# The FFN norms of a macaron transformer block: sums over features by products with ones, in place of transposes

## The chip, the cores and the metric

The kernel runs on one core of a Trainium2 chip. A time is the device time of one execution in microseconds (us). Three runs of the kernel before took 961.36, 961.11 and 961.50 us; their median is 961.36 us. One further execution was profiled, and all rows shown come from it.

In the rows, PE is TensorE's matrix products and PEld its weight loads, DVE is VectorE, ACT is ScalarE, POOL is GpSimd and SP is SyncE, which issues most transfers. L106 is line 106 of the kernel.

## The reference

The input is one sequence of 512 tokens with 1024 features in float32. The block is a "macaron": half an FFN, a mixer with two kinds of sparse attention, half an FFN, and a last norm.

```python
def rmsnorm(x, g):
    y = x * rsqrt(mean(x * x, axis=-1) + 1e-6)
    return y * g

def swiglu(h, w_gate, w_up, w_down):          # 1024 -> 2816 -> 1024
    return (silu(h @ w_gate) * (h @ w_up)) @ w_down

x = x + 0.5 * swiglu(rmsnorm(x, norm_ffn1), w_ffn1_gate, w_ffn1_up, w_ffn1_down)
x = x + hybrid_mixer(rmsnorm(x, norm_mix), ...)
x = x + 0.5 * swiglu(rmsnorm(x, norm_ffn2), w_ffn2_gate, w_ffn2_up, w_ffn2_down)
out = rmsnorm(x, norm_final)
```

The change concerns the first and the third `rmsnorm`, those ahead of the two FFNs.

## The kernel before

**Layout.** The activations stay on the chip as eight tiles `xs[k]` of 128 features x 512 tokens: features lie on the partitions, tokens along the free dimension. A sum over features, which a norm needs, is therefore a sum over eight tiles and then over 128 partitions.

**Precision.** Every matrix product is made from halves: a float32 operand is split into `hi`, the value rounded to the type float32r by ScalarE (a copy), and `lo`, the rest, by a subtraction on VectorE. `mm3` (lines 105 to 109) then makes three products, hi by hi (L106), hi by lo (L107) and lo by hi (L108); `mm2` makes two where one operand is exact. Weights are split in `halves` (hi at L95, lo at L99), the plain FFN blocks into `whi` and `wlo` with five buffers each.

**The norm.** The gain of the norm goes into the activations when they are split (`gained`, L162 and L163). The factor of each token, one over the root of the mean square, is applied behind the product, since it is the same for all features. `squares` (L175 to L179) squares each tile on ScalarE and adds the squares on VectorE into `acc`, 128 x 512, which still has to be summed over partitions. `rms` does that: four transposes of 128x128 on TensorE (L192) into the PSUM tile `pr`, so that tokens lie on partitions; a sum along the free dimension on VectorE (L193) into `rc`, 128x4; root on ScalarE (L194) and reciprocal on VectorE (L195) on these 128x4 values; four more transposes (L198), of `rc` spread over 128 columns, into the PSUM tile `pR`; and a copy by ScalarE (L200) into `R`, 128 x 512, where every partition holds the factors of all 512 tokens. `rms` is called three times: for both FFN norms and for the mixer's, which also uses `rc` itself.

**The FFN.** The 2816 hidden features are 22 blocks of 128. The first four (f = 0 to 3) are computed by `plain`: per block a product with the gate's weights (m = 0) and one with the up weights (m = 1), each of eight steps k of three products, 24 products of 128x512 into one PSUM tile `pgu`. `finish` multiplies both by R (L312), takes silu (L313), multiplies (L314) and splits the result into `h` (`kept`, L281 and L282). The 18 other blocks are computed in pairs by a Winograd scheme of seven half-width products (`pair`), whose right-hand operands are sums of blocks of the normed x; `sums_of_x` (L238 to L243) and `blocks_of_x` make them on VectorE and ScalarE from `xs` and R while TensorE works on the plain blocks. `down` makes the products back to 1024 features, group by group, between the others.

**What sets the order.** The kernel is written with a tile framework that plans the order of each engine's instructions at build time with a simulated timeline and priorities; the engines then run their own queues in that order and wait on semaphores. `tc.high_priority()` raises a block's priority in the planner. `tc.issue_after(ins)` makes what the block contains, on the engine of `ins`, stand behind `ins` in that engine's queue. `go` runs through the list of steps and calls a stage's parts with different leads. The norm's places are set by `rms_at`, which maps a step (f, m, k) to an instruction that it has to stand behind: the product of f = 1, m = 0, k = 4 stands behind the last transpose of `acc`, and the first product of m = 1 behind the last transpose of `rc`. In the first FFN `rms` is called in `after(0)`, behind the first product of the FFN and `squares`; in the second one also in `after(0)`, while the squares of x are made by the mixer's last job (`w_out`).

PSUM has eight banks, used as four tags (s, t, o, mm) of two buffers each; `pt(None, ...)` takes the four tags in turn. The SBUF tag `h` has 16 buffers. `wake` (L621 to L625) is a dozen products of a matrix of ones with itself at the very start, which keep TensorE at work until data arrive; the ones are set by VectorE in float32 and cast to float32r (L621).

Of the kernel before, what the change touches and what calls it, by code (L numbers as in the profile page):

```python
# [9 lines left out]
F32 = mybir.dt.float32  # L10
F32R = mybir.dt.float32r
AF = mybir.ActivationFunctionType
ALU = mybir.AluOpType
AX = mybir.AxisListType

S = 512
D = 1024
# [12 lines left out]
def block_kernel(ctx: ExitStack, tc: tile.TileContext, A: dict, out: bass.AP):  # L30
# [7 lines left out]
    nc = tc.nc  # L38

    cp = ctx.enter_context(tc.tile_pool(name="cp", bufs=1))  # L40
# [7 lines left out]
    def pt(tag, name):  # L48

        if tag is None:  # L50
            tag = ("s", "t", "o", "mm")[turns[0] % 4]
            turns[0] += 1
        return ps.tile([128, S], F32, name=name, tag=tag, bufs=2)

    def f32(ap):
        return ap.bitcast(F32)
# [62 lines left out]
    def mm2(p, w, v, first, last):  # L119

        nc.tensor.matmul(p, w, v[0], start=first, stop=False)
        return nc.tensor.matmul(p, w, v[1], start=False, stop=last)
# [17 lines left out]
    eps = cp.tile([128, 1], F32, name="eps")  # L140
# [6 lines left out]
    tabs = cp.tile([33, 16], F32, name="tabs")  # L147
    far = cp.tile([32, 16], F32, name="far")
    cp.tile([128, 48], F32, name="rest")
    ones_f = cp.tile([128, 128], F32, name="ones_f")  # L150
    nc.vector.memset(ones_f, 1.0)
    ident = cp.tile([128, 128], F32, name="ident")
    make_identity(nc, ident)

# [1 line left out]
    made = [None]  # L156
# [10 lines left out]
    R = cp.tile([128, S], F32, name="R")  # L167
    rc = cp.tile([128, NT], F32, name="rc")

    acc = cp.tile([128, S], F32, name="acc")  # L170
# [11 lines left out]
    summed = [None]  # L182
    turned_R, copied_R = [None], [None]

    def rms(ptag):


        with tc.high_priority():
            p = pt(ptag, "pr")
            for i in range(NT):  # L190
                b = slice(i * 128, (i + 1) * 128)
                summed[0] = nc.tensor.transpose(p[:, b], acc[:, b], ident)  # L192
            nc.vector.tensor_reduce(rc, p.rearrange("p (i n) -> p i n", i=NT), AX.X, ALU.add)  # L193
            nc.scalar.activation(rc, rc, AF.Sqrt, bias=eps, scale=1.0 / D)  # L194
            nc.vector.reciprocal(rc, rc)  # L195
            p = pt(ptag, "pR")
            for i in range(NT):
                turned_R[0] = nc.tensor.transpose(p[:, i * 128:(i + 1) * 128],  # L198
                                                  rc[:, i:i + 1].to_broadcast([128, 128]), ident)
            copied_R[0] = nc.scalar.activation(R, p, AF.Copy)  # L200


    HT = S // 2

    class Ffn:
# [14 lines left out]
        def __init__(self, wg, wu, which, tmp, hp, sp):  # L220
            self.w, self.which, self.tmp, self.hp, self.sp = (wg, wu), which, tmp, hp, sp
            self.xg, self.hs, self.steps = None, {}, []
            self.b, self.temps = {}, {}
            self.last_lo = None
            self.x_made = None
            self.waiting = []
            self.in_pair = None
            self.runs, self.left = 0, 0
            self.rms_at = {}
            self.th, self.tl = [sp.tile([128, 4, 3, HT], F32R, name=n, tag=n, bufs=1) for n in ("th3", "tl3")]  # L230
            sp.tile([128, 16], F32, name="gap", tag="gap", bufs=1)

# [52 lines left out]
        def plain(self, f):  # L285

            got = {}

            def loads(m):
                if first_w:  # L290
                    got[m] = first_w.pop(0)
                else:
                    got[m] = chunk((8, 128))
                    fetch(got[m], self.w[m][f])

            def halves_of(m):
                with tc.issue_after(self.x_made.ins) if self.x_made and m else nullcontext():
                    got[m] = halves(got[m])
                if self.x_made and m:
                    self.x_made, self.first_up = None, last_hi[0]  # L300

            def run(m):
                p = got["p", m] = pt(None, "pgu")
                for k in range(NK):
                    gate = self.rms_at.get((f, m, k))
                    with tc.issue_after(gate[0].ins) if gate else nullcontext():
                        mm3(p, got[m][k], self.xg[k], k == 0, k == NK - 1)

            def finish():
                t = [self.t("t") for _ in range(2)]  # L310
                for m in range(2):
                    nc.vector.tensor_tensor(t[m], got["p", m], R, ALU.mult)  # L312
                self.silu = nc.scalar.activation(t[0], t[0], AF.Silu)  # L313
                nc.vector.tensor_tensor(t[1], t[1], t[0], ALU.mult)  # L314
                self.kept(f, t[1])

            return [[lambda m=m: loads(m), None, lambda m=m: halves_of(m), lambda m=m: run(m), finish if m else None]
                    for m in range(2)]

# [294 lines left out]
    with ExitStack() as ph:  # L614
        tmp = ph.enter_context(tc.tile_pool(name="tmp1", bufs=5))
        hp = ph.enter_context(tc.tile_pool(name="hp1", bufs=2))
        sp = ph.enter_context(tc.tile_pool(name="sp1", bufs=2))


        ones = hp.tile([128, S], F32R, name="ones", tag="h", bufs=16)[:, :128]  # L620
        nc.vector.tensor_copy(ones, ones_f)  # L621
        wake = pt(None, "wake")
        for _ in range(12):
            nc.tensor.matmul(wake.rearrange("p (a b) -> p a b", a=4), ones,
                             ones.unsqueeze(1).to_broadcast([128, 4, 128]), start=True, stop=True)  # L625
        nc.scalar.activation(R[:, 0:1], eps, AF.Sqrt)
        ffn = Ffn(A["wg1"], A["wu1"], 0, tmp, hp, sp)
        ffn.xg = [gained(k, 0) for k in range(NK)]
        ffn.x_made = made[0]
        ffn.rms_at = {(1, 0, 4): summed, (1, 1, 0): turned_R}  # L630

        make_rows = bias_rows(hp)

        def after(i):
            if i == 0:
                with tc.issue_after(ffn.first_up.ins):
                    for k in range(NK):
                        squares(hp, k, "h", 16)
                rms(None)
            if i == 3:  # L640
                make_rows()
            if 3 <= i < 7:
                ffn.sums_of_x(i - 3)
            if i == 7:
                for k in range(4):
                    ffn.blocks_of_x(k)
            if i == 38:
                for h0 in range(0, 16, 2):
                    h = slice(h0, h0 + 2)
                    row = scr_r[h]  # L650
                    with behind_fetched():
                        fetched[0] = nc.sync.dma_start(
                            scr_t[h].rearrange("h p w -> p h w"),
                            bass.AP(tensor=row.tensor, offset=row.offset, ap=[[0, 128], [RVW, 2], [1, RVW]]))
            if i >= 70 and i % 8 == 0 and (i - 72) // 8 < 8:
                a = (i - 72) // 8
                row = scr_c[0:1, :]
                with behind_fetched():
                    for j in range(NT):
                        nc.sync.dma_start(  # L660
                            cb[a * 16:(a + 1) * 16, j],
                            bass.AP(tensor=row.tensor, offset=row.offset + 31 - 8 * j - a,
                                    ap=[[CMW, 16], [16 * CMW, 8], [1, 32]]))

        xg = []

        def then(d, p):
            if d == 0:
                with tc.issue_after(ffn.silu.ins):
                    nc.scalar.activation(rc[:, 0:1], eps, AF.Sqrt)  # L670
            half_added(d, p)
            xg.append(gained(d, 1))
            squares(tmp, d, "tmp", 5)

        ffn.lay(A["wd1a"])
        ffn.steps += ffn.down(A["wd1b"], range(NF - NF % FP, NF), then, (None,), (4, 2, 2), left=0)
        ffn.go(after)


    with ExitStack() as ph:  # L680
# [538 lines left out]
        for pair in range(4):  # L1219
            for odd in range(2):  # L1220
                h = 8 + 2 * pair + odd
# [29 lines left out]
    with ExitStack() as ph:  # L1251
        tmp = ph.enter_context(tc.tile_pool(name="tmp3", bufs=5))
        hp = ph.enter_context(tc.tile_pool(name="hp3", bufs=2))
        sp = ph.enter_context(tc.tile_pool(name="sp3", bufs=2))
        ffn = Ffn(A["wg2"], A["wu2"], 2, tmp, hp, sp)
        ffn.xg = xg
        ffn.rms_at = {(1, 0, 4): summed, (1, 1, 0): turned_R}
        hs = ffn.hs

        def after(i):  # L1260
            if i == 0:
                rms(None)
            if 3 <= i < 7:
                ffn.sums_of_x(i - 3)
            if i == 7:
                for k in range(4):
                    ffn.blocks_of_x(k)
# [68 lines left out]
        for i in range(NT):  # L1336
            b = slice(i * 128, (i + 1) * 128)
            for half in range(2):
                parts = [slice(0, S)] if (i, half) != (NT - 1, 1) else [slice(0, HT), slice(HT, S)]
                for n, cols in enumerate(parts):  # L1340
                    p = pt(None, "pd")[:, cols]
# [112 lines left out]
```

## Time and profile before

| what | value |
|---|---|
| median of three runs | 961.36 us (961.11 to 961.50) |
| span of the profiled execution | 958.68 us (958.7 on its page) |
| mean granted TensorE clock | 0.998 |
| busy: PE, DVE, ACT, POOL | 949.7, 764.6, 563.2, 163.2 us |
| instructions | 18276, of them 6703 products |
| first FFN norm: last addition into `acc`, first use of R | ends at 20.4, starts at 25.7 us |
| second FFN norm: the same | ends at 627.2, starts at 633.1 us |

The profile's span runs from the first to the last instruction; 2.68 us of the median lie outside it. A row of a timeline gives the start in us from the span's start, the duration, the engine, the line, the operation, the tiles (out<-in) and shapes; "x4" are four in a row, and a bracket tells of idle time before it and who ended it. A row of a group gives, behind the bar, the busy time of all its instructions and the mean duration of one in ns. A row of waits gives the total, the count and the longest in us. Products of PE overlap in their pipeline, so the distance between two starts says more than a duration.

### The profile page before, as it was taken

To read this page: it belongs to the slowest core of one execution; us is meant where nothing else is said; L and a number is where in the kernel's file an instruction comes from. 1 tells how busy PE (TensorE), PEld (TensorE's weight loads), DVE (VectorE), ACT (ScalarE), POOL (GpSimd) and SP (SyncE) were. 2 spreads that over 40 slices of the span, in tenths; PEclk is the share of its full clock that TensorE was granted. 3 is DMA by queue.
4 is the path that set the end of the run, shared out by engine and by line. 5 is a ranking of instruction groups with operands and counts; after the bars stand their busy time and mean duration, and the time that the engine had idled before them with its cause. 6 is when DMAs were issued, how large, how long until landed. Compare 5 with 4: busy or idle time off the path is not lost.

```text
span 958.7 us, 18276 instructions
## 1 busy us (share of the span) xinstructions
PE 949.7 (99%) x6703; PEld 879.8 (92%) x6703; DVE 764.6 (80%) x1596; ACT 563.2 (59%) x1170; POOL 163.2 (17%) x209
## 2 busy tenths in 40 slices
PE   9999999999999999999999999999999999999997
PEld 7889999999999989889888888888999999999985
DVE  7998897688777588967788677889889788778954
ACT  6565555454554356778877887655565545545443
POOL 2000000000000000056778897100000000000002
PEclk9999999999999999999999999999999999999999
DMA  8447444333321226551312332236334321425442
GB/s 283 128 166 235 140 133 135 113 92 95 106 68 57 60 67 179 163 160 35 90 38 72 92 96 73 66 106 224 130 114 132 131 79 56 133 51 123 92 154 88
DMA packets 70138, 109.17 MB, mean 114 GB/s; under 512 B 27518, under 2 KB 34127, under 8 KB 70049
## 3 DMA queue, kind: packets, MB, share of 16 engines
q1 hardware_dynamic: 69232, 106.68, 36.1%
q8 instruction: 52, 0.85, 0.4%
q0 software_dynamic: 384, 0.55, 0.3%
q10 hardware_dynamic: 432, 0.79, 0.2%
q14 instruction: 38, 0.30, 0.1%
HBM read 100.44 MB, written 7.40 MB: 112 GB/s over the span
## 4 chain that ended last, share of the span: by engine, by line
PE 97%; DVE 1%; DMA 1%; ACT 0%; issue 0%; POOL 0%; POOLq 0%; SPq 0%; DVEq 0%; ACTq 0%
PE pd L116 14%; PE pu L108 7%; PE pu L106 7%; PE pu L107 7%; PE pw L106 5%; PE pw L108 5%; PE pw L107 5%; PE pd L107 4%; PE pd L108 4%; PE pd L106 4%; PE ps_s L1070 3%; PE pgu L107 3%; PE pgu L108 3%; PE pgu L106 3%; PE pp L106 3%; PE pp L108 3%
## 5 line engine op out<-in xcount | busy, mean ns | idle before, releaser
L249 ACT ACTIVATE sph<-aw 128x512 fp32r<-128x512 f32 x252 | 157.9, 631 | 193.7 <-issue 71.9
L250 DVE TENSOR_TENSOR spl<-aw,sph 128x512 fp32r<-128x512 f32 x252 | 171.2, 684 | 55.2 <-ACT sph L249 53.3
L95 ACT ACTIVATE whi<-raw 128x512 fp32r<-128x512 f32 (+2 forms) x198 | 119.2, 614 | 85.0 <-PE pd L116 25.3
L116 PE MATMUL pd<-h,whi 128*128 128x256 f32 x784 | 120.7, 276 | 0.0
L99 DVE TENSOR_TENSOR wlo<-raw,whi 128x512 fp32r<-128x512 f32 (+1 forms) x162 | 106.8, 669 | 16.1 <-ACT whi L95 15.9
L108 PE MATMUL pu<-th,spl 128*128 128x256 f32 x432 | 119.3, 276 | 0.0
L106 PE MATMUL pu<-th,sph 128*128 128x256 f32 x432 | 119.2, 276 | 0.0
L107 PE MATMUL pu<-tl,sph 128*128 128x256 f32 x432 | 119.2, 276 | 0.0
L116 PEld LDWEIGHTS pd<-h,whi 128*128 128x128 f32 x784 | 103.5, 188 | 0.1
L335 DVE TENSOR_TENSOR aw<-aw 128x512 f32<-128x512 f32 x144 | 98.2, 682 | 0.0
L106 PEld LDWEIGHTS pu<-th,sph 128*128 128x128 f32 x432 | 81.1, 188 | 1.3
L107 PEld LDWEIGHTS pu<-tl,sph 128*128 128x128 f32 x432 | 81.1, 188 | 1.2
L108 PEld LDWEIGHTS pu<-th,spl 128*128 128x128 f32 x432 | 81.1, 188 | 0.0
L108 PE MATMUL pw<-xo,spl 128*128 128x256 f32 x288 | 79.6, 276 | 0.0
L106 PE MATMUL pw<-xo,sph 128*128 128x256 f32 x288 | 79.4, 276 | 0.0
L107 PE MATMUL pw<-xo,sph 128*128 128x256 f32 x288 | 79.4, 276 | 0.0
L116 PE MATMUL pd<-h,wlo 128*128 128x256 f32 x392 | 76.3, 276 | 0.0
L612 DVE SCALAR_TENSOR_TENSOR x<-pd,x 128x512 f32<-128x512 f32 x80 | 54.3, 682 | 14.7 <-PE pd L116 12.4
L1354 POOL TENSOR_SCALAR mean<-ss 128x1 f32<-128x1 f32 x4 | 1.4, 343 | 343.5 <-ACT sqd L1314 343.4
L116 PEld LDWEIGHTS pd<-h,wlo 128*128 128x128 f32 x392 | 59.0, 188 | 0.0
L991 POOL MEMSET tb<- 128x256 f32 x16 | 4.9, 312 | 311.4 <-DVE x L612 310.4
L106 PEld LDWEIGHTS pw<-xo,sph 128*128 128x128 f32 x288 | 54.1, 188 | 1.7
(271 smaller groups left out, 2707.3 us busy)
## 6 DMA issues: line engine op xcount, KB each, us to landing
aw<-in_wg SPq DMA_DIRECT2D x72, 256.0 KB, 4.3
aw<-in_wu SPq DMA_DIRECT2D x72, 256.0 KB, 4.8
raw<-in_wd1a SPq DMA_DIRECT2D x20, 512.0 KB, 3.9
raw<-in_w_a SPq DMA_DIRECT2D x16, 512.0 KB, 3.7
raw<-in_wd2a SPq DMA_DIRECT2D x16, 512.0 KB, 3.6
raw<-in_w SPq DMA_DIRECT2D x8, 512.0 KB, 4.7
raw<-in_w_o SPq DMA_DIRECT2D x8, 512.0 KB, 3.6
raw<-in_wg SPq DMA_DIRECT2D x7, 512.0 KB, 3.5
```

What stands on the lines that cost most here:

```text
L95: last_hi[0] = nc.scalar.activation(hi, v, AF.Copy)
L99: nc.vector.tensor_tensor(lo, v, f32(hi), ALU.subtract)
L106: nc.tensor.matmul(p, w[0], v[0], start=first, stop=False, skip_group_check=again)
L107: nc.tensor.matmul(p, w[0], v[1], start=False, stop=False, skip_group_check=again)
L108: newest[0] = nc.tensor.matmul(p, w[1], v[0], start=False, stop=last, skip_group_check=again)
L116: nc.tensor.matmul(p[:, h], a, b[:, h], start=first and n + i == 0, stop=last and n == 2, skip_group_check=True)
L249: nc.scalar.activation(hi, v, AF.Copy)
L250: self.last_lo = nc.vector.tensor_tensor(lo, v, f32(hi), ALU.subtract)
L335: nc.vector.tensor_tensor(to, x, y, op)
L612: nc.vector.scalar_tensor_tensor(xs[d], p, 0.5, xs[d], ALU.mult, ALU.add)
L991: nc.gpsimd.memset(t[:, :S - 256], 0.0)
L1070: latest[0] = nc.tensor.matmul(to, q, k, start=part == at, stop=part != at)
```

## The change

Both FFN norms use a new function, `rms_everywhere`. It splits `acc` into halves and multiplies both, with two products of 128x512, by a 128x128 matrix of ones: each partition of the result then holds the sum over all partitions for each of 512 tokens. The root (with the division by 1024 and the epsilon) and the reciprocal are taken on the 128x512 tile, straight into R. The mixer's norm keeps `rms`.

With it come: the matrix of ones is set once, in float32r, and the cast goes; the two places in `rms_at` change (k = 7 in the first FFN and k = 5 in the second, and the m = 1 product now stands behind the same sums); in the second FFN the function is called ahead of all steps instead of in `after(0)`, with a root on one column placed behind the last `gained` so that the root's table is loaded there, and the weight splits of f = 2 stand behind the copy (m = 0) and the root (m = 1).

```diff
-    ones_f = cp.tile([128, 128], F32, name="ones_f")
-    nc.vector.memset(ones_f, 1.0)
+    ones = cp.tile([128, 128], F32R, name="ones")
+    nc.vector.memset(f32(ones), 1.0)
...
+    def rms_everywhere(hp):
+        with tc.high_priority():
+            hi, lo = [hp.tile([128, S], F32R, name="h", tag="h", bufs=16) for _ in range(2)]
+            first = nc.scalar.activation(hi, acc, AF.Copy)
+            nc.vector.tensor_tensor(lo, acc, f32(hi), ALU.subtract)
+            p = pt(None, "pr")
+            summed[0] = mm2(p, ones, (hi, lo), True, True)
+            root = nc.scalar.activation(R, p, AF.Sqrt, bias=eps, scale=1.0 / D)
+            nc.vector.reciprocal(R, R)
+        return first, root
...
-            self.rms_at = {}
+            self.rms_at, self.halves_at = {}, {}
...
             def halves_of(m):
-                with tc.issue_after(self.x_made.ins) if self.x_made and m else nullcontext():
+                behind = self.x_made if self.x_made and m else self.halves_at.get((f, m))
+                with tc.issue_after(behind.ins) if behind else nullcontext():
                     got[m] = halves(got[m])
...
-        ones = hp.tile([128, S], F32R, name="ones", tag="h", bufs=16)[:, :128]
-        nc.vector.tensor_copy(ones, ones_f)
...
-        ffn.rms_at = {(1, 0, 4): summed, (1, 1, 0): turned_R}
+        ffn.rms_at = {(1, 0, 7): summed, (1, 1, 0): summed}
...
-                rms(None)
+                rms_everywhere(hp)
...
-        ffn.rms_at = {(1, 0, 4): summed, (1, 1, 0): turned_R}
+        ffn.rms_at = {(1, 0, 5): summed, (1, 1, 0): summed}
         hs = ffn.hs
+        with tc.issue_after(made[0].ins):
+            nc.scalar.activation(rc[:, 0:1], eps, AF.Sqrt)
+        first, root = rms_everywhere(hp)
+        ffn.halves_at = {(2, 0): first, (2, 1): root}
 
         def after(i):
-            if i == 0:
-                rms(None)
```

## The prediction

> **What bounds the kernel now.** I read first the page's shares and its chain, then TensorE's waits, then the order of time around the four groups of transposes.
>
> ```profile
> PE 949.7 (99%) x6703; PEld 879.8 (92%) x6703; DVE 764.6 (80%) x1596; ACT 563.2 (59%) x1170; POOL 163.2 (17%) x209
> ...
> PE 97%; DVE 1%; DMA 1%; ACT 0%; issue 0%; POOL 0%; POOLq 0%; SPq 0%; DVEq 0%; ACTq 0%
> ```
>
> ```profile
> PE wake L624 <- DVE ones L621: 1.5, 1, 1.5
> PE ps_s L1070 <- DMA kst<-kst: 0.4, 1, 0.4
> PE pgu L107 <- DVE xo L163: 0.3, 1, 0.3
> ```
>
> TensorE (PE) is busy for 949.7 of 958.7 us and is 97% of the chain. Only 2.2 us of waits are listed for the whole execution, 1.5 of them before its first product. So a microsecond taken out of PE's stream after the start comes off the end, and one that another engine gains is worth nothing; a delay elsewhere costs only what exceeds PE's supply of finished operands. The profiled execution has 958.68 us of span; the median of the runs is 961.36, 2.68 us more, which I take as lying around the span and unchanged.
>
> **What leaves PE and what comes.** Below are rows in order of time, PE alone: start, duration, then the group.
>
> ```profile
> 20.09 0.39 PE L108 MATMUL pgu<-xo,wlo 128*128 128x512 f32 x1
> ...
> 20.77 0.40 PE L108 MATMUL pgu<-xo,wlo 128*128 128x512 f32 x1
> 21.00 0.60 PE L192 MATMUL pr<-ident,acc 128*128 128x128 f32 x4
> 21.35 0.48 PE L106 MATMUL pgu<-xo,whi 128*128 128x512 f32 x1
> 21.67 0.39 PE L107 MATMUL pgu<-xo,whi 128*128 128x512 f32 x1
> ...
> 631.52 0.39 PE L108 MATMUL pgu<-xo,wlo 128*128 128x512 f32 x1
> 631.75 0.60 PE L198 MATMUL pR<-ident,rc 128*128 128x128 f32 x4
> 632.10 0.48 PE L106 MATMUL pgu<-xo,whi 128*128 128x512 f32 x1
> 632.41 0.39 PE L107 MATMUL pgu<-xo,whi 128*128 128x512 f32 x1
> ```
>
> Durations overlap, so I go by starts. From 20.09 to 20.77 stand three 512-column products: 0.227 us each. From the L108 before the transposes to the second product behind them is 0.90 us in the first norm and 0.89 in the second; two products alone would be 0.454. Four transposes so cost 0.44 to 0.45 us, part of it the slow product behind them. Two norms have four such groups: 4 x 0.445 = 1.78 us leave. What comes is two products with ones per norm. They have the shape of the rows beside them, 128x512 with a 128x128 stationary matrix, so 4 x 0.227 = 0.91. Net on PE: **-0.87 us**. From below, the new products might be exposed like the one behind a transpose (0.31 to 0.32): 4 x 0.32 = 1.28, net -0.50.
>
> **What the other engines get.** Groups by form: count, then busy us and mean ns.
>
> ```profile
> L99 DVE TENSOR_TENSOR wlo<-raw,whi 128x512 fp32r<-128x512 f32 x152 | 102.9, 686 | 15.5 <-ACT whi L95 15.3
> L193 DVE TENSOR_REDUCE rc<-pr 128x4 f32<-128x512 f32 x3 | 2.1, 686 | 0.0
> L195 DVE RECIPROCAL rc<-rc 128x4 f32<-128x4 f32 x3 | 0.5, 173 | 0.2 <-ACT rc L194 0.2
> L1147 DVE RECIPROCAL mc<-mc 128x8 f32<-128x8 f32 x4 | 0.8, 197 | 0.0
> L1319 DVE RECIPROCAL ss<-ss 128x1 f32<-128x1 f32 x4 | 0.7, 164 | 1.0 <-ACT ss L1318 1.0
> L200 ACT ACTIVATE R<-pR 128x512 f32<-128x512 f32 x3 | 1.8, 599 | 0.2 <-PE pR L198 0.2
> L194 ACT ACTIVATE rc<-rc,eps 128x4 f32<-128x4 f32 x3 | 0.9, 292 | 1.1 <-DVE rc L193 1.1
> L178 ACT ACTIVATE sq<-x 128x512 f32<-128x512 f32 x21 | 12.3, 616 | 0.0
> ```
>
> ScalarE (ACT) loses 0.29 + 0.60 and gets a copy to `hi` (0.62, as the square) and a root on 128x512 out of PSUM (0.60, as the copy of R): +0.3 us a norm, and it is 59% busy. VectorE (DVE) loses 0.69 + 0.17 and gets the subtraction for `lo` (0.69) and a **reciprocal on 128x512**, which no row shows. Its lower bound is any pass over 128x512, 0.69 us. Above: from 1 to 8 elements it grows from 164 to 197 ns, 4.7 ns an element; from 4 to 8, 6.0 ns. By these, 512 take 2.6 and 3.2 us. I take 3.0, call it r, and keep 0.7 and 3.2.
>
> [...]
>
> **Whether DVE's extra time reaches PE.** First DVE's load behind each norm (columns: length, PE, PEld, DVE, ACT, POOL busy), then when the sum of squares ends and when R is first used.
>
> ```profile
> 25.70:76.90 51.20, 51.20 (x258) 43.38 (x257) 51.18 (x97) 30.63 (x60) 0.00 (x0) 1.00 0.39 137
> 632.50:687.30 54.80, 54.80 (x286) 47.02 (x285) 54.28 (x103) 32.44 (x63) 0.00 (x0) 1.00 0.42 140
> ```
>
> ```profile
> 19.68 0.68 DVE L179 TENSOR_TENSOR acc<-acc,sq 128x512 f32<-128x512 f32 x1
> ...
> 25.69 1.29 DVE L312 TENSOR_TENSOR t<-pgu,R 128x512 f32<-128x512 f32 x2
> ...
> 625.07 2.14 DVE L179 TENSOR_TENSOR acc<-acc,sq 128x512 f32<-128x512 f32 x3
> ...
> 633.11 1.29 DVE L312 TENSOR_TENSOR t<-pgu,R 128x512 f32<-128x512 f32 x2
> ```
>
> DVE is full for 51.18 of 51.20 us from the first use of R, and for 54.28 of 54.80 in the second FFN. Nothing takes up a late start of that stretch, so everything that DVE makes in it comes later by as much. How much: from the end of `acc` the new chain is the copy 0.62, the subtraction 0.69, the two products 0.23 + 0.39, the root 0.60 and r, with five handovers of about 0.06: 2.83 + r. One weight remainder (0.6 by the spacing of starts) stands before R's first use. First norm: 20.36 + 3.43 + r = 26.8 against 25.69, so 1.1 us later. Second: 627.21 + 3.43 + r = 633.6 against 633.11, so 0.5 later; the old chain had lost more there.
>
> Most of what DVE makes is ready long before PE asks: counted in order, the tenth weight remainder ends at 23.25 for a product at 33.95. The exception is the low half of the fourth plain feature block `h`, in the rows from 62.57 on:
>
> ```profile
> 22.57 0.68 DVE L99 TENSOR_TENSOR wlo<-raw,whi 128x512 fp32r<-128x512 f32 x1
> ...
> 33.95 0.39 PE L108 MATMUL pgu<-xo,wlo 128*128 128x512 f32 x1
> ...
> 62.57 0.68 DVE L282 TENSOR_TENSOR h<-t,h 128x512 fp32r<-128x512 f32 x1
> 62.73 1.29 PE L106 MATMUL pd<-h,whi 128*128 128x512 f32 x5
> ...
> 64.10 0.39 PE L107 MATMUL pd<-h,whi 128*128 128x512 f32 x1
> ...
> 669.99 0.68 DVE L282 TENSOR_TENSOR h<-t,h 128x512 fp32r<-128x512 f32 x1
> ...
> 670.98 0.39 PE L107 MATMUL pd<-h,whi 128*128 128x512 f32 x1
> ```
>
> It ends 0.85 us before L107 needs it in the first FFN, and 0.31 before in the second. If the order of products stays, PE stalls for 1.1 - 0.85 = 0.25 and 0.5 - 0.3 = 0.2 us, 0.45 in all. The order needn't stay: the planner lays it out anew, and already here it puts five products with the high half ahead while the low half is missing; if it prices the reciprocal it puts more. I take half, **+0.23 us**, with 0 and 0.9 (at r = 3.2) as ends.
>
> **Edits at nothing.** The new products wait for `lo`, and what is queued behind them on PE are the products of f = 1. `lo` can be ready 1.43 us after `acc`: at 21.8 and 628.6. The gates moved from k = 4 to 7 and 5, so the latest places are some three and one triples (0.68 us each) behind the old ones: 21.00 + 2.04 = 23.0 and, by the second group's own start, 628.56 + 0.68 = 629.2. Cover is 1.2 and 0.6 us; if DVE finishes another remainder first (0.6), the second is used up. The root's table load, moved ahead of the second norm, costs ACT 1.28 us where it stood idle anyway:
>
> ```profile
> 623.54 0.63 ACT L95 ACTIVATE whi<-raw 128x512 fp32r<-128x512 f32 x1 [1.86 <-PE pgu L107]
> ...
> 628.07 1.15 ACT L95 ACTIVATE whi<-raw 128x512 fp32r<-128x512 f32 x2 [3.90 <-PE pgu L107]
> 629.24 1.28 ACT L194 ACT_TABLE_LOAD   x1
> ```
>
> ACT idles 1.86 and 3.90 us there, waiting only for PE to free weight buffers, which is also why holding the weights of f = 2 behind the copy and the root costs nothing; were ACT full there, the sum of squares would end up to 1.28 us later. No DMA is issued or moved, so SP's and POOL's queues stay as they are; the taken-out cast before the wake-up products starts these some 0.25 us earlier, but the first real products wait for DVE's `xo` (the third row of PE's waits), so nothing follows. One PSUM tile less per norm shifts the rotation of banks: every bank is asked for in another turn, and each stays two turns from its last use; without that distance PE would wait for one eviction, some 0.7 us.
>
> **Sum.** 958.68 - 0.87 + 0.23 = 958.04 us of span; 961.36 - 0.64 = **960.7 us**.
>
> **The rivals.**
> A, on the slower side: *the long reciprocal makes the low half of `h` late*, with the order unchanged. The stalls are (r - 1.9 - 0.85) + (r - 2.45 - 0.3), about 2(r - 2.75), against -0.87: the kernel is slower than before from r = 3.2, and slower by 1.9 us from r = 4.15. From there on rows give no bound. For it: DVE without slack, leads of 0.85 and 0.31. Against: small rows that grow by 4.7 to 6 ns, and a planner that fills. [...]
> B: *PE stands at the new products* because `lo` is behind remainders on DVE: one remainder or two, 0.6 to 1.2 us over the cover in one norm: 961.3. For it: two remainders in a row at the place of the first norm (the row below). Against: the block has high priority.
>
> ```profile
> 20.37 1.27 DVE L99 TENSOR_TENSOR wlo<-raw,whi 128x512 fp32r<-128x512 f32 x2
> ```
>
> C: *the products are no cheaper than the transposes*, that is, PE's stream isn't shortened: 961.4. Against it: the spacing of like products over the whole FFN.
> D: *more is gained than PE's rows say*, because another order shortens the tail: the row below is the last product, and 6.8 us lie between its end (951.9) and the end of the span. The time is 959.2 if 1.5 us of them goes. Nothing in the profile asks for that.
>
> ```profile
> 951.63 0.28 PE L108 MATMUL pd<-sph,h 128*128 128x256 f32 x1
> ```
>
> **How the numbers follow.** A measurement of this kernel tells about 0.2%, 1.9 us, from no change: 959.4 to 963.3. Chances: forecast with stalls of 0 to 0.7 us (960.4 to 961.1) 0.54; A 0.18, of which 0.09 beyond 963.3; B 0.11; C 0.06; D 0.07, nearly all beyond 959.4; the rest, small changes of order, 0.04. So faster 0.07, slower 0.09, the same 0.84. The range takes in the forecast, B, C and the half of A that is near: 959.7 to 962.6.
>
> **What would show it.** Right: PE about 0.9 us less busy; the two products 0.22 to 0.24 us apart in start; R's first use 0.5 to 1.5 us after its old places relative to `acc`; a reciprocal of 2.6 to 3.2 us; no wait of PE on `h`, `hi` or `lo` above 0.5 us. Wrong: a reciprocal near 0.7 (then nothing stalls, 960.5) or above 4 (then A), a new PE wait of more than 1 us, or a span that moves by more than 2 us, which no step here explains.

## The result and the profile after

The changed kernel takes 967.21 us (median of five runs, 966.22 to 967.81) against 961.30 us for the kernel before on the same chip: a ratio of 1.0061, 95% interval 1.005 to 1.0072. It is 5.9 us slower, where 960.7 with a range up to 962.6 was forecast.

First the page of the changed kernel, its shares and its chain, and under it TensorE's waits (total, count, longest in us).

```profile
PE 950.3 (98%) x6691; PEld 879.1 (91%) x6691; DVE 771.0 (80%) x1595; ACT 562.4 (58%) x1171; POOL 164.2 (17%) x209
...
PE 91%; DVE 5%; ACT 1%; issue 1%; DMA 0%; POOL 0%; POOLq 0%; ACTq 0%; DVEq 0%
```

```profile
PE pd L107 <- DVE h L295: 2.5, 2, 1.3
PE wake L636 <- DVE ones L151: 1.1, 1, 1.1
PE pv L106 <- ACT sph L262: 0.9, 2, 0.5
PE ps_s L1082 <- DVE aq L734: 0.7, 1, 0.7
```

DVE, which had 1% of the chain, now has 5%, and PE waits twice for the low half of `h`. PE's busy time on the page did not fall (950.3 after 949.7): products on either side of a stall don't overlap with their neighbours, which start 0.23 us apart, and are booked with their full 0.39 to 0.50 us. Without the stalls it is 948.8, as a page further down shows.

Next the two norms in order of time: VectorE's rows and the products with ones.

```profile
19.31 0.68 DVE L179 TENSOR_TENSOR acc<-acc,sq 128x512 f32<-128x512 f32 x1
...
21.28 0.67 DVE L208 TENSOR_TENSOR h<-acc,h 128x512 fp32r<-128x512 f32 x1
...
24.39 3.35 DVE L212 RECIPROCAL R<-R 128x512 f32<-128x512 f32 x1 [1.63 <-ACT R L211]
27.66 1.22 DVE L99 TENSOR_TENSOR wlo<-raw,whi 128x512 fp32r<-128x512 f32 x2
28.80 1.28 DVE L326 TENSOR_TENSOR t<-pgu,R 128x512 f32<-128x512 f32 x2
...
627.62 2.12 DVE L179 TENSOR_TENSOR acc<-acc,sq 128x512 f32<-128x512 f32 x3
630.52 0.69 DVE L208 TENSOR_TENSOR h<-acc,h 128x512 fp32r<-128x512 f32 x1 [0.78 <-ACT h L207]
...
633.63 3.35 DVE L212 RECIPROCAL R<-R 128x512 f32<-128x512 f32 x1 [0.75 <-ACT R L211]
...
637.44 1.27 DVE L326 TENSOR_TENSOR t<-pgu,R 128x512 f32<-128x512 f32 x2
```

```profile
22.77 0.40 PE L108 MATMUL pgu<-xo,wlo 128*128 128x512 f32 x1
23.00 0.39 PE L121 MATMUL pr<-h,ones 128*128 128x512 f32 x1
23.24 0.40 PE L122 MATMUL pr<-h,ones 128*128 128x512 f32 x1
23.47 0.40 PE L106 MATMUL pgu<-xo,whi 128*128 128x512 f32 x1
```

From the end of `acc` (19.99 and 629.74) to the first use of R now pass 8.81 and 7.70 us, where before it was 5.33 and 5.90: R is 3.5 and 1.8 us later. In between the reciprocal takes 3.35 us, and in the first norm `lo` is ready at 21.95 while the products with ones start only at 23.00, right ahead of the product of k = 7, which has to stand behind them: that is the latest place that this gate leaves them. The two start 0.24 us apart and the next product 0.23 us behind them. In the second norm they start at 631.78 and 632.48, with two other products between them and the same spacing from one product to the next.

What that lateness does to TensorE stands around 64 and 673 us, and once more at 702 us, where the high half of a pair's weights (`sph`) is late.

```profile
62.23 1.29 PE L106 MATMUL pd<-h,whi 128*128 128x512 f32 x5
64.87 0.50 PE L107 MATMUL pd<-h,whi 128*128 128x512 f32 x1 [1.34 <-DVE h L295]
...
671.70 1.29 PE L106 MATMUL pd<-h,whi 128*128 128x512 f32 x5
674.10 0.50 PE L107 MATMUL pd<-h,whi 128*128 128x512 f32 x1 [1.11 <-DVE h L295]
...
702.36 0.39 PE L106 MATMUL pv<-xo,sph 128*128 128x256 f32 x1 [0.54 <-ACT sph L262]
```

As before, five products with the high half are put ahead, and then PE stands. Measured as the excess of starts over the spacing of like products, including the slow products right behind: 3.0 us at the two `h`, 1.7 us at the pairs (75.8, 92.4 and 701.5 us), and 0.3 us more than before at a score product at 406 us.

The last part is the end of the span. First the kernel before, whose last product starts at 951.63: the second of ScalarE's squares (`sqd`) of the last token blocks, and two rows of GpSimd. Then the same of the changed kernel, with its last product.

```profile
944.95 0.63 ACT L1314 ACTIVATE sqd<-x 128x512 f32<-128x512 f32 x1 [2.75 <-DVE x L1313]
...
951.35 1.28 POOL L1353 TENSOR_TENSOR zg<-x,gf 128x512 f32<-128x512 f32 x1
952.71 0.51 POOL L1354 TENSOR_SCALAR mean<-ss 128x1 f32<-128x1 f32 x1
```

```profile
952.04 0.63 ACT L1328 ACTIVATE sqd<-x 128x512 f32<-128x512 f32 x1 [5.27 <-DVE x L1327]
...
956.20 0.28 PE L108 MATMUL pd<-sph,h 128*128 128x256 f32 x1
...
956.35 1.80 POOL L1370 TENSOR_TENSOR x<-x,gf 128x512 f32<-128x512 f32 x1
958.12 1.71 POOL L1367 TENSOR_TENSOR zg<-x,gf 128x512 f32<-128x512 f32 x1
959.91 0.25 POOL L1368 TENSOR_SCALAR mean<-ss 128x1 f32<-128x1 f32 x1
```

GpSimd's `mean`, on which the last output waits, comes 1.08 us after the start of the last product before, and 3.71 us after it now. GpSimd's order is the same in both kernels, but it runs later against TensorE: ScalarE's second square starts 4.16 us ahead of the last product where it started 6.68 us ahead, since it stands idle for 5.27 us, not 2.75, until VectorE has added to its `x`. That addition is the second of VectorE's last additions before and the fourth now. So two multiplications of GpSimd, which moreover take 1.80 and 1.71 us where they took 1.30 and 1.28, fall behind the start of the last product. From the last product's start to the end of the span it is 958.68 - 951.63 = 7.05 us before and 965.62 - 956.20 = 9.42 now: the tail is **2.37 us longer**. (The expectations below count it from the product before the last, 0.11 more.)

So the span grew by 6.94: 4.57 up to the last product (3.0 + 1.7 + 0.3 - 0.9 = 4.1 of it named, 0.5 in small gaps that I did not assign), and 2.37 behind it. The medians differ by 5.9 because the profiled execution of before was 0.8 us quicker than its median, and that of the changed kernel (967.49) 0.3 us slower: in runs whose own span is known an execution of either kernel lies about 1.85 us above it (not 2.68, as was taken ahead of the prediction), and 958.68 + 1.85 = 960.5.

### The profile page after: what moved, and what is told of

It is laid out like the page before. It is cut to its first block, busy times and chain, and to the rows that moved or that the text cites. A ratio compares the mean times of both kernels' runs of the same rounds, so it can differ in the third digit from the quotient of the medians.

```text
span 965.6 us, 18262 instructions
## 1 busy us (share of the span) xinstructions
PE 950.3 (98%) x6691; PEld 879.1 (91%) x6691; DVE 771.0 (80%) x1595; ACT 562.4 (58%) x1171; POOL 164.2 (17%) x209
## 4 chain that ended last, share of the span: by engine, by line
PE 91%; DVE 5%; ACT 1%; issue 1%; DMA 0%; POOL 0%; POOLq 0%; ACTq 0%; DVEq 0%
PE pd L116 14%; PE pu L106 7%; PE pu L107 7%; PE pu L108 7%; PE pw L106 5%; PE pw L107 5%; PE pw L108 5%; PE ps_s L1082 3%; PE pp L106 3%; PE pp L108 3%; PE pp L107 3%; PE pv L106 3%; PE pv L108 3%; PE pd L107 3%; PE pv L107 3%; PE pd L108 3%
```

## The experiments

In all kernels with a reciprocal on 64 of the 512 columns, the other factors stay roots, so that only the time is of use. Medians of the kernel before, taken with each group on the same chip, are 961.45 (first four), 961.06 (next four) and 961.14 us (last two).

**The reciprocal made short in the changed kernel.**

```diff
-            nc.vector.reciprocal(R, R)
+            nc.vector.reciprocal(R[:, :64], R[:, :64])
```

> The changed kernel, with the reciprocal taken on 64 of the 512 columns of R only (the other columns keep the root, so the result is not the reference's). Theory: the reciprocal of 3.35 us on VectorE starts everything behind it late, and TensorE then waits for the low half of the fourth plain block h (1.5 and 1.3 us) and for later pair weights (0.3 to 0.7 us each). Without most of the reciprocal these waits go: some 4 us less than the changed kernel's 967.2, about 963; the end behind the last product stays as long as there (9.5 us). Rival, turned banks: the shifted turn of the PSUM banks alone gives another order with these waits in it; then they stay and the time stays near 967. Rival, dear products: the two products cost TensorE as much as the transposes; then the time stays about 1 us above what the theory gives.

963.14 us (962.3 to 964.39; ratio 1.0018, 1.0009 to 1.0027). The waits of PE in this kernel:

```profile
PE ps_s L1082 <- DMA kst<-kst: 0.6, 1, 0.6
PE pv L106 <- ACT sph L262: 0.6, 1, 0.6
```

The waits on `h` are gone, and with them 4.1 of the 5.9 us. What is left, 1.7 us, isn't the length of the reciprocal; the tail is unchanged (9.43 us).

**One turn of banks more behind each norm**, so that the PSUM tags that follow come in the turn of before: first in the changed kernel, then together with the short reciprocal.

```diff
             nc.vector.reciprocal(R, R)
+            turns[0] += 1
```

> The changed kernel, with the turn of the PSUM tags moved on by one inside rms_everywhere, so that all later tiles take the banks that they took before. Theory: the waits on h stay (2.5 us or so in the list of waits), and the end behind the last product goes back from 9.5 to about 7.2 us: 967.2 - 2.4 = 964.8. Rival, turned banks: waits and end both go back, 960.5 to 961. Rival, late end: the longer end comes from VectorE's lateness, not from the turn; then the time stays near 967.

> Both edits together (reciprocal on 64 columns only, so the result is not the reference's, and the old turn of the banks). Theory: no wait on h, the end as before, and TensorE's 0.87 us are left: 960.4. Rival, dear products: 961.3 or more. Rival, late end: as e1, about 963.

967.76 us (966.9 to 968.53; ratio 1.0068, 1.0055 to 1.008) and 964.14 us (962.28 to 964.98; ratio 1.0026, 1.0016 to 1.0035): both miss their texts. The tail is 7.1 us in both, as before. But the planner also laid out the second norm anew: the product with ones waits 2.1 us for `hi` in both (row of the first; below it two windows of 3.41 us: length, then busy us of PE, PEld, DVE, ACT, POOL, then PE's granted clock).

```profile
629.91 0.50 PE L121 MATMUL pr<-h,ones 128*128 128x512 f32 x1 [2.12 <-ACT h L207]
```

```profile
627.60:631.01 3.41, 1.29 (x6) 0.92 (x6) 2.49 (x5) 1.33 (x3) 0.00 (x0) 1.00 0.49 163
631.01:634.43 3.42, 3.42 (x10) 2.64 (x9) 0.17 (x1) 0.00 (x0) 0.00 (x0) 0.50 0.09 35
```

So the tail came back, and what it gave was spent on a new stall, in the first of the two with 3.42 us at half clock (0.50) behind it. The edit does not do one thing only, and the two times alone settle nothing.

**The same shift of turns given to the kernel before**, which has nothing else of the change.

```diff
                 rms(None)
+                turns[0] -= 1
```

> The kernel before, with the turn of the PSUM tags set back by one behind each FFN norm, as the change does it; nothing else is changed. Theory: no wait on h, but the end behind the last product grows by some 2.4 us: 963.7. Rival, turned banks: the whole loss, 967. Rival, late end: 961.3, as before.

976.93 us (974.62 to 977.34; ratio 1.0159, 1.0145 to 1.0173), far from all three texts: 15.5 us slower by a line, the same in both FFNs, that emits no instruction. PE waits 4.1 us for weights from 12.9 us on, resumes at half clock (0.50), and waits 2.6 us more for `acc` from 633.1 us on. Its tail is long as well (10.35 us), with ScalarE's second square idle for 5.27 us as in the changed kernel.

```profile
12.00:17.00 5.00, 0.94 (x5) 0.44 (x3) 4.42 (x8) 5.00 (x11) 3.13 (x5) 0.93 1.01 372
17.00:22.00 5.00, 4.96 (x12) 3.72 (x13) 3.68 (x9) 1.03 (x2) 0.00 (x0) 0.50 0.83 186
```

The turn in which PSUM tags are taken is an input to the planner's whole order. To separate the tail, the turn has to be shifted where only the tail can follow.

**The turn put right ahead of the last eight token blocks only**: in the changed kernel, in it with the short reciprocal, and, as the opposite, put wrong in the kernel before. By lines and tiles, TensorE's order stays as it was in all three, up to the last 20 products.

```diff
         last, zg = range(NF - NF % FP, NF), {}
+        turns[0] += 2
```

> The changed kernel, with the turn of the PSUM tags moved on by two ahead of the last eight token blocks only, so that these take the banks of the kernel before and nothing earlier is ordered anew. Theory: the end behind the last product falls from 9.5 to 7.2 us and the waits on h stay: 967.2 - 2.4 = 964.8. Rival, late end (the longer end is VectorE's lateness): 967.

> As e5, with the reciprocal on 64 of the 512 columns only (so the result is not the reference's). Theory: what is left of the change is TensorE's saving, some pair-weight waits of 0.8 us and nothing else: 963.1 - 2.4 = 960.7. Rival, dear products: above 961.4. Rival, late end: 963.1.

> The kernel before, with the turn of the PSUM tags moved on by two ahead of the last eight token blocks only: they take the banks that the changed kernel gives them. Theory: the end behind the last product grows from 7.2 to 9.5 us, all else stays: 961.4 + 2.4 = 963.8. Rival, late end: 961.4.

964.71 us (963.84 to 966.04; ratio 1.0041, 1.0029 to 1.0054), 960.35 us (959.42 to 961.55; ratio 0.9993, 0.9985 to 1.0002) and 964.10 us (963.75 to 965.28; ratio 1.0034, 1.0021 to 1.0048), each within 0.4 us of its text. The last product of the first starts here (its span ends at 962.03, 7.06 us later), and that of the third here (962.27, 9.45 later):

```profile
954.97 0.28 PE L108 MATMUL pd<-sph,h 128*128 128x256 f32 x1
```

```profile
952.82 0.28 PE L108 MATMUL pd<-sph,h 128*128 128x256 f32 x1
```

The turn of banks makes the long tail, in either kernel: it takes 2.5 us from the changed kernel (967.21 to 964.71) and puts 3.0 on the one before. The runs of the first spread from 963.84 to 966.04, so some 1 us of a difference with it can be noise; in the profiles the tails differ by 2.36 and 2.40 us. The waits on `h` are untouched by it (2.5 us in 2). With both repaired, PE waits for nothing longer than 0.4 us once it has begun. The page's shares of that kernel and its longest wait:

```profile
PE 948.8 (99%) x6691; PEld 878.5 (92%) x6691; DVE 765.2 (80%) x1595; ACT 563.9 (59%) x1171; POOL 161.7 (17%) x209
```

```profile
PE ps_s L1082 <- DMA kst<-kst: 0.4, 1, 0.4
```

PE is busy 0.9 us less than before. From the first to the second of the three, 4.4 us are the price of a full-length reciprocal, together with the other order that the planner lays out for it inside the FFNs. The short one takes 0.55 us (two of them in place of two long ones are most of the 5.8 us by which DVE's busy time falls, from 771.0 to 765.2), and with it R is not late: it is first used 4.96 and 4.46 us after `acc`, sooner than the 5.33 and 5.90 of before.

**The reciprocal on ScalarE**, as exp(-0.5 ln(..)), with the tail put right, so that VectorE gets none. The two roots on one column that load the table ahead become logarithms too.

```diff
-            root = nc.scalar.activation(R, p, AF.Sqrt, bias=eps, scale=1.0 / D)
-            nc.vector.reciprocal(R, R)
+            nc.scalar.activation(R, p, AF.Ln, bias=eps, scale=1.0 / D)
+            root = nc.scalar.activation(R, R, AF.Exp, scale=-0.5)
```

> As e5, with root and reciprocal on ScalarE alone: the logarithm of the mean square, then the exponential of minus half of it, two passes over 128x512 and one more table load, and no reciprocal on VectorE. Theory: VectorE gets 0.2 us less work per norm than before the change, R comes some 2 us earlier than with the reciprocal, no wait on h: 960.4 to 960.8. Rival, ScalarE's passes and table loads take the reciprocal's place: waits of TensorE on weights or on h stay, 962 or more.

962.31 us (961.91 to 963.19; ratio 1.0016, 1.0007 to 1.0024): 2.4 us better than with VectorE's reciprocal, and 2.0 short of the short one. ScalarE's rows in the first norm:

```profile
24.15 0.69 ACT L211 ACTIVATE R<-pr,eps 128x512 f32<-128x512 f32 x1 [2.03 <-PE pr L122]
24.74 0.62 ACT L95 ACTIVATE whi<-raw 128x512 fp32r<-128x512 f32 x1
25.38 1.28 ACT L212 ACT_TABLE_LOAD   x1
26.67 0.63 ACT L212 ACTIVATE R<-R 128x512 f32<-128x512 f32 x1
```

A weight's high half and a table load stand between the two passes, and R is first used 6.41 us after `acc`, still 1.1 later than before. PE waits 0.4 us on `h` and 0.7 on `sph`. The text's 960.4 to 960.8 is missed, and its rival (962 or more) gives the time. Lateness of R is not enough to explain it: in the second norm R is first used 5.84 us after `acc`, no later than before, and yet PE loses 1.2 us there at `h` and at a pair's weights. Which of ScalarE's added passes and table loads makes these late was not separated.

**The reciprocal alone, added to the kernel before**, behind the copy into R, its result unused.

```diff
-            copied_R[0] = nc.scalar.activation(R, p, AF.Copy)
+            copied_R[0] = nc.scalar.activation(R, p, AF.Copy); ptag or nc.vector.reciprocal(acc, R)
```

> The kernel before, with its transposes and its order of banks, and one reciprocal of 128x512 more on VectorE behind the copy into R of each FFN norm; its result goes into a tile that nobody reads, so the output is that of before. In VectorE's order it stands right ahead of the first use of R, as it does after the change. Theory (the time of the reciprocal on a full VectorE is what makes h late): R's first use 3.35 us later in both norms; with the leads of 0.85 and 0.31 us and an unchanged order the stalls are 2.5 + 3.0 = 5.5 us, so 961.3 + 5.5 = 966.8 at most and, with what the planner fills, 964 to 966.8; PE waits on h again and the tail stays at 7.2 us. Rival (the reciprocal alone is harmless, it is the products, the gates and the other order of the norm that cost): under 962.3, no wait on h above 0.5 us.

968.71 us (967.53 to 969.41; ratio 1.0077, 1.0063 to 1.0091), 7.6 us slower: above even the 966.8 that I gave as the most. VectorE around the first norm, TensorE at the late `h`, and two windows:

```profile
25.42 3.35 DVE L200 RECIPROCAL acc<-R 128x512 f32<-128x512 f32 x1
28.69 1.22 DVE L312 TENSOR_TENSOR t<-pgu,R 128x512 f32<-128x512 f32 x2
```

```profile
62.55 1.29 PE L106 MATMUL pd<-h,whi 128*128 128x512 f32 x5
65.70 0.38 PE L106 MATMUL pw<-xo,sph 128*128 128x256 f32 x1 [1.85 <-ACT sph L249]
65.92 0.28 PE L107 MATMUL pw<-xo,sph 128*128 128x256 f32 x1
66.24 0.50 PE L107 MATMUL pd<-h,whi 128*128 128x512 f32 x1
```

```profile
63.34:66.75 3.41, 1.51 (x7) 0.84 (x6) 3.41 (x8) 0.82 (x2) 0.00 (x0) 1.00 0.00 0
66.75:70.16 3.41, 3.41 (x9) 2.66 (x9) 3.41 (x7) 3.19 (x7) 0.00 (x0) 0.50 0.00 0
```

R's first use is 3.1 and at least 3.3 us later from `acc` than before (in the second norm the reciprocal ends 9.2 us after it). The stalls behind it are 2.5 us in the first FFN and 1.7 + 1.3 us (`h` and pairs) in the second, 5.5 as by the leads; but 1.6 us come on top from products at half rate behind the first stall (0.43 us apart where they were 0.23, for 3.41 us), and 0.7 at the score product. No product with ones, no moved gate and no other turn of banks is in this kernel: the reciprocal, with the order that the planner lays out for it, is enough. Here the planner did put another product into the gap, two of `pw`, but their own operand was late too.

**The products with ones one step earlier** in the first FFN, with the tail put right.

```diff
-        ffn.rms_at = {(1, 0, 7): summed, (1, 1, 0): summed}
+        ffn.rms_at = {(1, 0, 6): summed, (1, 1, 0): summed}
```

> The changed kernel with the old turn of banks in the last eight token blocks, and the products with ones of the first FFN one step earlier (gate k = 6 in place of 7), 0.68 us earlier in TensorE's queue. Theory (lateness of R in the first norm goes one to one into the stalls behind it, and the gate held the products 1.05 us after lo was ready): R's first use 0.7 us earlier from the end of acc, stalls of the first FFN 0.7 us less, 964.7 - 0.7 = 964.0. Rival (VectorE's remainders ahead of the reciprocal set its place, not the gate): R's first use within 0.3 us of its old place and 964.7.

```profile
24.11 3.35 DVE L212 RECIPROCAL R<-R 128x512 f32<-128x512 f32 x1 [0.51 <-ACT R L211]
27.38 0.63 DVE L99 TENSOR_TENSOR wlo<-raw,whi 128x512 fp32r<-128x512 f32 x1
27.93 1.27 DVE L326 TENSOR_TENSOR t<-pgu,R 128x512 f32<-128x512 f32 x2
```

964.15 us (963.72 to 964.64; ratio 1.0031, 1.002 to 1.0043). R is first used 7.10 us after `acc` in place of 8.59 with k = 7 and the same tail: 0.9 from the idle time ahead of the reciprocal and 0.6 because one remainder, not two, stands before the use. So the gate did hold R. The stalls of the first FFN fall from 2.2 to 1.7 us only, those of the second change by 0.6 the other way, and the times (964.71 and 964.15) have overlapping intervals: that the gate's place is worth 0.7 us of the whole is not shown.

None of the versions that compute the same beats the kernel before.

## Why the prediction was wrong

**What held.** TensorE's own account: the products are 0.23 to 0.24 us apart (0.227 forecast), and with the two losses taken out PE is 0.9 us less busy and the time 0.7 us under that of before (960.35 against 961.06; the interval just touches no change), as "net -0.87" has it. DVE as the place of the loss, the low half of the fourth plain `h` as the product that waits, and its leads of 0.85 and 0.31 us were right too: with R 3.5 and 1.8 us later they give 2.6 + 1.5 = 4.1 us, and 4.4 was the price measured. Place by place the agreement is looser, and in part luck: the stalls are 2.5 and 2.2 us in the two FFNs, and only 3.0 of these 4.7 us stand at `h`. The products with ones wait for nothing, the table load is hidden (1.28 us at 622.41, behind which ScalarE still idles for 1.13 and 3.14 us), and the earlier wake-up products bring nothing in the rows.

**First failed step: "1.1 us later" and "0.5 later" for R.** They measured 3.5 and 1.8. The price of the reciprocal is the smaller part of this: 3.35 against 3.0, just above the upper row bound of 3.2; 3352 ns for 512 elements are 6.55 ns each, where the small rows grow by 4.7 and 6.0. No run shows an r of 4.15 or more, on which rival A's chance of 0.09 beyond 963.3 stood: the two reciprocals of the changed kernel take 3.35 us each. The larger part was in my own text: the chain from `acc` was summed as if the products ran when `lo` is ready, at 21.8 and 628.6, while two paragraphs on their places were put at 23.0 and 629.2 and the difference was booked as "cover 1.2 and 0.6 us". What is cover for PE is lateness for R. In the run the products started at 23.00, 1.05 us after `lo`, and `lo` itself, behind two remainders on VectorE, was ready 1.96 us after `acc` in place of 1.43. A second remainder ahead of R's use (some 0.5) and a root of 0.69 in place of 0.60 complete it in the first norm. In the second norm the last product with ones starts 2.74 us after `acc`, where the sum has it at 1.7. With the gates in the sum, and r = 3.0, my own rows would have given 23.0 + 0.62 + 0.60 + 3.0 + 0.6 and some 0.15 of handovers, 28.0 against 25.69, so 2.3 us, and in the second norm 634.2 against 633.11, so 1.1: stalls of 1.45 + 0.8 and 961.36 - 0.87 + 2.2 = 962.7.

**Second: "I take half", since the planner fills.** It didn't: the five products ahead of the wait are the same as before (62.23 and 671.70), and the next PE instruction is the one that waits. In the kernel with only the reciprocal it did fill, with products whose operands were late too: with DVE full (busy for 4.00 of 4.00 us in each stretch from 58 to 74 us), what could fill hung on it as well. The leads beyond `h` that I called long gave way as well: pairs at 75.8, 92.4 and 701.5 us cost 1.7.

**Third: the rotation of banks "at nothing".** The term was priced as a wait on a bank, and there is none: the loss is that the planner orders the last token blocks differently when their PSUM tags come in another turn, so that the block that ScalarE squares second is finished later, and GpSimd's chain to the last `mean` with it. Shifting the turn at that place moves the tail by 2.4 us in both kernels (2.5 off and 3.0 on in the medians). Rival D held that another order could shorten the tail; that it could lengthen it by as much was not weighed.

**Rival A** was the right mechanism with the wrong size: its formula 2(r - 2.75) gives 1.2 at r = 3.35 and so 961.7, because it carried the same lateness. The account of the medians: -0.7 (products for transposes) + 4.4 (late R) + 2.5 (tail) = +6.2; measured was +5.9 in the first comparison. The three are steps of one path from kernel to kernel, so that they add up by construction; what is shown by each is its size.

**Still open:** why the planner takes the order with the longer tail, whose timeline the profile doesn't show, and how much of the pairs' stalls belongs to lateness and how much to their new order.

## What to carry to other kernels

When a gate sets a step's place in an engine's queue, put that place into both sums: the time by which the gate covers a wait of one engine is added to the chain of whoever needs the result. Where an engine is full behind the edit, convert its extra time into stalls one to one over the smallest lead as a first estimate, before any credit for refilling: here that gave 4.1 for 4.4 us, against 0.9 us of savings, and 5.5 of the 7.6 us of the added reciprocal. And where a build-time planner chooses the order, an edit that only shifts the allocation of buffers is a change of order everywhere behind it: compare the orders of the tail, and measure the shift by itself.

## What the runs showed that was not expected

A reciprocal of 128x512 in float32 takes 3.35 us on VectorE, 4.9 times the 0.68 us of a subtraction of that size; from the 197 ns row for 8 elements it grows by (3352 - 197) / 504 = 6.3 ns an element, and 64 elements take 0.55 us.

After some stalls TensorE goes on at half rate, with products 0.43 us apart where they were 0.23, and after others of equal length it doesn't. Five stalls with the granted clock around them:

| kernel | stall of PE | PE busy around it | granted clock there | granted clock right behind |
|---|---|---|---|---|
| turn put back | 2.12 us, up to 629.91 | 1.29 of 3.41 us from 627.60 | 1.00 | 0.50 from 631.01 to 634.43 |
| reciprocal added to the kernel before | 1.85 us, up to 65.70 | 1.51 of 3.41 us from 63.34 | 1.00 | 0.50 from 66.75 to 70.16 |
| turn shifted in the kernel before | 4.1 us, from 12.9 on | 0.94 of 5.00 us from 12.00 | 0.93 | 0.50 from 17.00 to 22.00, then 0.86 to 26.00 |
| turn put back, short reciprocal | 2.1 us | 2.56 of 4.00 us from 624.00, 3.33 of 4.00 from 628.00 | 1.00 and 1.00 | 1.00 to 632.00 |
| changed kernel | 1.34 us, up to 64.87 | 3.52 of 4.00 us from 60.00, 3.13 of 4.00 from 64.00 | 1.00 and 1.00 | 1.00 to 68.28 |

The stretch at half clock costs some 1.6 us on top of the stall in the first two: 3.41 us of products 0.43 us apart in place of 0.23. In the third it is about twice as long, 6.8 us (an estimate from the clocks of its three stretches: 0.7 us at half clock make 0.93 of the first, 5.0 the second and 1.1 make 0.86 of the third). The first and the fourth kernel wait equally long for `hi`, and only the first goes on at half clock, so the length of a stall alone doesn't tell. What decides it was not shown.

The nine executions of the kernel with the turn put back and the short reciprocal are four of 962.3 to 963.3 us with a mean clock of 0.998 to 0.999 and five of 964.1 to 965.0 with 0.997, as one stretch of 3.41 us more at half clock would make (an estimate: half of 3.41 us is 0.0018 of 961 us).
